# RWKV in two chains with PSUM of their own: inverses of a block and preparation of the next interleaved with the chunks of the preceding one

## The chip, the cores and the metric

The kernel runs on one core of a Trainium2 chip. A core has five engines that run their own instruction streams: TensorE (PE, matrix products, whose results go to PSUM), VectorE (DVE), ScalarE (ACT), GpSimd (POOL) and SyncE (SP), whose queue issues nearly all DMAs here. The metric is the device time of one execution in microseconds (us). Lower is better.

## The reference

One layer of a hybrid trunk, batch 1, 2048 tokens and 16 learned meta tokens ahead of them (2064 in all), width 1024, float32. The normalised input goes through one projection, whose columns feed three head groups:

```python
p = rms_norm(h, norm_mix_pre[l]) @ w_in[l]
pa = p[..., :A_COLS]
pb = p[..., A_COLS:A_COLS + B_COLS]
pc = p[..., A_COLS + B_COLS:]
oa = rg_lru_group(...)               # linear recurrence with gates, 256 columns
ob = forgetting_attention_group(...) # softmax attention with decay, 8 heads of 64
oc, v_own = rwkv7_group(...)         # RWKV-7, 4 heads of 64
mixed = jnp.concatenate([oa, ob, oc], axis=-1) @ w_out[l]
h = h + rms_norm(mixed, norm_mix_post[l])
f = causal_dwconv(rms_norm(h, norm_ffn_pre[l]) @ ffn_up[l], ffn_conv[l])
gate, val = jnp.split(f, 2, axis=-1)
f = (jax.nn.gelu(gate, approximate=True) * val) @ ffn_down[l]
h = h + rms_norm(f, norm_ffn_post[l])
```

The RWKV group is a recurrence over tokens with a 64 x 64 state for each head:

```python
def step(S, inp):
    r_t, w_t, k_t, v_t, kk_t, a_t = inp
    s_kk = jnp.einsum('bhij,bhj->bhi', S, kk_t)
    S = S * w_t[:, :, None, :] - s_kk[..., None] * (kk_t * a_t)[:, :, None, :] + v_t[..., None] * k_t[:, :, None, :]
    return S, jnp.einsum('bhij,bhj->bhi', S, r_t)
```

## The kernel before

The kernel has these stages: the input projection, with gates, RWKV and LRU beside it; the attention, in two halves of its query blocks; the output projection `w_out_tile`, partly beside the second half of the attention; and the two products of the feed-forward block (`ffn_up`, `Down`), which the change doesn't touch.

**Input projection.** The tokens go through in three parts (`w_in_tokens`): two blocks of tokens each, of 400 and 384, 384 and 384, 256 and 256 columns. `w_in_part` (L293) is a generator whose steps are called units here, 25 in a part: first the gates' columns (`w_in_gate`), then 8 units of RWKV's columns ("c"), 4 of the LRU's ("a"), and the keys, values and queries. A unit makes 24 matmuls for each block of tokens into a `psp` tile (five PSUM banks on the left side). The results are stored to DRAM scratch, where the recurrences read them.

**Recurrences beside it.** `Beside` (L1897) holds a generator and a pace: after each unit, `advance` takes PACE steps of it. PACE is 2.0, and the generator of a part, `recurrences` (L1927), is added after READY + 1 = 14 units. What isn't done at a part's end goes on in the next part's units; what is left after the last part is traced by `finish` before the attention. The generator takes the attention's gates (`gate_block`, L377), and then for each of three blocks of 256 tokens (block 8 has 64):

- preparation (`Rwkv.block`, L993): loads of the mixed columns, decay, gates, normalised keys; its results are `rav` (r, -, v), `bk`, `wc`, `bon`, `sg`;
- in `Rwkv.chunks` (L1077) up to `SOLVED`: scores of a chunk's 64 tokens (L1096, masked into `sc` at L1101), their 16 x 16 diagonal blocks through DRAM (`da`, L1114, L1117) into rows on which POOL and DVE solve 15 steps in turn (L1139, L1140), the result back through DRAM (`dx`, L1143), and transposes of `bk` and `rav` (L1125) into `sc` and `w3`;
- then the rest of `chunks` of the *preceding* block, kept as `R.ending`: inverses put together from the 16 x 16 blocks (`small`, L1163), products per chunk (L1203 to L1227), the state from chunk to chunk (L1247), the outputs (L1280, L1284), group norm, and at the end the transposes (L1304), the gate product (L1308) and the store to `scr["mix"]` (L1318);
- the LRU of the block (`lru_block`, L1371), in four steps.

**PSUM of the recurrences.** `ps()` gives tiles of the tag "at" with two buffers (named `rps` in the profile), `pe()` tiles of the tag "ae" with one (named `eps`). Tiles of a tag take its buffers in the order of the program. Preparation, gates and LRU use `pe()`; scores, transposes, chunks and output use `ps()`.

**Order.** A planner with a timeline model sets the order of the instructions on each engine at compile time, from the order of the program as priority and from what is ready by its model. On the chip each engine takes its instructions in that order and waits on semaphores. PSUM and SBUF of the recurrences are on the right side and come free when `rec` closes; weights of W_out take that room in SBUF, and the attention's third bank for maxima (`ps_more`, used from the sixth head of the first half on) that room in PSUM. `meta()` (L579), the attention of the meta tokens, is traced at the half turn of the attention.

## Time and profile before

| what | time |
|---|---|
| runs, median of 3 (lowest to highest) | 3083.14 us (3079.87 to 3085.98) |
| the profiled execution | 3087.03 us |
| its span, from the first to the last instruction | 3085.3 us |
| granted clock of TensorE, mean | 0.964 |

Times on a profile's rows are microseconds from the start of the span unless marked ns. The profile's page has a row for each engine: busy time, share of the span, number of instructions. Below it the span stands in 40 slices of 77.1 us; a digit is the busy share of a slice in tenths, and PEclk the clock that was granted to TensorE, in tenths of full speed. A window's row gives start and end of the stretch, its length, the busy time of each engine (count), then the granted clock, the share of time in which the DMA engines were busy, and what they moved in GB/s. A row of the timeline gives start, length, engine, line, operation, what it writes and reads, and a count of equal ones merged. A row of waits gives who waited for whom: us in total, times, the longest. A fp32 matmul stands as two matmul records. A busy PE is one that has a matmul under way; that doesn't make it PE at its peak.

### The profile page before, as it was taken

The numbers are of one execution on the slowest core, as the hardware profiler recorded it, in microseconds if no ns is written. First come the engines' busy times: TensorE is split into PE (matmuls) and PEld (weight loads), VectorE is DVE, ScalarE is ACT, GpSimd is POOL, SyncE is SP. The second block draws the span as 40 slices with busy tenths as digits, with TensorE's granted clock in tenths as the row PEclk, the third lists the DMA queues.
The fourth block names the chain that finished last, engine by engine and source line by source line (L and its number), as shares of the span: only waits on it lengthen the run. The fifth ranks groups of instructions, "written<-read, shape, count | busy, mean of one in ns | idle before, by whom it ended". The sixth has DMA issues, their size and how long they took to land.

```text
span 3085.3 us, 52708 instructions
## 1 busy us (share of the span) xinstructions
PE 2905.6 (94%) x18470; PEld 2485.8 (81%) x18470; DVE 2127.9 (69%) x4349; ACT 1447.5 (47%) x2783; POOL 1317.4 (43%) x1491
## 2 busy tenths in 40 slices
PE   7999999999989878898989899999999999999998
PEld 6998899888866544565458899999999998787876
DVE  5268544766677867777745788788778776547766
ACT  4245322444335534445534656666566665324333
POOL 1001121122134645546742457445645534556665
PEclk9999999999978979999999999999999999999999
DMA  6776457466653345445235555566777765435444
GB/s 216 244 229 215 148 176 221 153 219 219 192 134 78 91 112 126 109 112 119 61 112 185 166 175 176 178 196 213 216 211 212 217 193 164 167 103 174 145 163 143
DMA packets 463210, 515.78 MB, mean 167 GB/s; under 512 B 84977, under 2 KB 355003, under 8 KB 461393
## 3 DMA queue, kind: packets, MB, share of 16 engines
q1 hardware_dynamic: 462560, 512.03, 55.5%
q8 instruction: 145, 2.38, 0.3%
q14 instruction: 121, 0.98, 0.1%
q0 software_dynamic: 384, 0.39, 0.0%
HBM read 360.73 MB, written 151.56 MB: 166 GB/s over the span
## 4 chain that ended last, share of the span: by engine, by line
PE 39%; DMA 5%; DVE 5%; POOL 3%; issue 2%; ACT 1%; SPq 0%; POOLq 0%; DVEq 0%; ACTq 0%
PE psu L168 9%; PE psu L169 9%; PE psu L170 8%; PE psd L170 2%; PE psd L169 2%; PE psd L168 2%; DMA u<-scr_ff 1%; PE po L696 1%; DMA xt<-scr_h 1%; PE pswo L168 1%; PE pswo L169 1%; PE pswo L170 1%; DVE fo L1571 1%; PE sc L673 1%; DVE uw L1571 1%
## 5 line engine op out<-in xcount | busy, mean ns | idle before, releaser
L168 PE MATMUL psu<-xo,uw 128*128 128x344 f32 x1848 | 591.3, 324 | 16.2 <-ACT xo L1570 6.9
L169 PE MATMUL psu<-xo,uw 128*128 128x344 f32 x1848 | 594.1, 322 | 0.5 <-DVE xo L1571 0.5
L170 PE MATMUL psu<-xo,uw 128*128 128x344 f32 x1848 | 584.3, 320 | 0.0
L170 PE MATMUL psp<-xh,wl 128*128 128x384 f32 (+2 forms) x1152 | 379.1, 330 | 3.8 <-DMA wl<-scr_wk 3.8
L168 PE MATMUL psp<-xh,wh 128*128 128x384 f32 (+2 forms) x1152 | 380.2, 330 | 2.3 <-DMA wh<-scr_wk 2.3
L169 PE MATMUL psp<-xl,wh 128*128 128x384 f32 (+2 forms) x1152 | 377.6, 328 | 0.0
L168 PEld LDWEIGHTS psu<-xo,uw 128*128 128x128 f32 x1848 | 348.1, 189 | 19.5 <-ACT xo L1570 7.1
L1571 DVE TENSOR_TENSOR uw<-uq,uw 128x512 fp32r<-128x512 f32 x341 | 311.1, 918 | 65.3 <-ACT uw L1570 62.4
L169 PEld LDWEIGHTS psu<-xo,uw 128*128 128x128 f32 x1848 | 349.2, 189 | 1.1 <-DVE xo L1571 1.0
L170 PEld LDWEIGHTS psu<-xo,uw 128*128 128x128 f32 x1848 | 347.6, 189 | 0.0
L1570 ACT ACTIVATE uw<-uq 128x512 fp32r<-128x512 f32 x462 | 288.0, 627 | 113.0 <-PE psu L170 53.8
L678 ACT ACTIVATE p<-sc,bias 128x512 f32<-128x512 f32 (+4 forms) x352 | 197.8, 590 | 238.2 <-PE sc L674 181.7
L1701 DVE SCALAR_TENSOR_TENSOR uy<-psu,ffn_cols,uy 128x342 f32<-128x342 f32 (+1 forms) x396 | 223.8, 566 | 67.3 <-ACT uy L1699 65.9
L717 POOL TENSOR_TENSOR acc<-acc,p 128x512 f32<-128x512 f32 (+3 forms) x208 | 223.8, 1082 | 65.2 <-DVE acc L717 40.4
L1707 POOL TENSOR_TENSOR uy<-uy,uy 128x342 f32<-128x342 f32 (+1 forms) x132 | 138.5, 1049 | 256.3 <-DVE uy L1701 72.1
L170 PEld LDWEIGHTS psp<-xh,wl 128*128 128x128 f32 x1152 | 219.5, 191 | 13.3 <-issue 6.3
L1571 POOL TENSOR_TENSOR uw<-uq,uw 128x512 fp32r<-128x512 f32 x121 | 175.6, 1451 | 125.9 <-ACT uw L1570 102.8
L168 PEld LDWEIGHTS psp<-xh,wh 128*128 128x128 f32 x1152 | 219.6, 191 | 8.5 <-issue 3.5
L169 PEld LDWEIGHTS psp<-xl,wh 128*128 128x128 f32 x1152 | 219.3, 190 | 6.8 <-issue 4.8
L548 DVE TENSOR_REDUCE mc<-mx 128x1 f32<-128x400 f32 (+6 forms) x320 | 171.7, 553 | 67.3 <-PE mx L545 62.5
L1571 DVE TENSOR_TENSOR fo<-u,fo 128x896 fp32r<-128x896 f32 x88 | 109.7, 1247 | 122.4 <-ACT fo L1570 122.4
L1570 ACT ACTIVATE fo<-u 128x896 fp32r<-128x896 f32 x88 | 81.1, 922 | 206.2 <-POOL u L1817 111.7
(460 smaller groups left out, 6474.0 us busy)
## 6 DMA issues: line engine op xcount, KB each, us to landing
uq<-scr_us SPq DMA_DIRECT2D x220, 256.0 KB
uq<-in_ffn_up_dram SPq DMA_DIRECT2D x209, 256.0 KB
wl<-scr_wk SPq DMA_DIRECT2D x48, 512.0 KB
wh<-scr_wk SPq DMA_DIRECT2D x48, 512.0 KB
u<-scr_ff SPq DMA_DIRECT2D x88, 256.0 KB
scr_ff<-uy SPq DMA_DIRECT2D x110, 171.0 KB
raw<-in_w_in_dram SPq DMA_DIRECT2D x24, 512.0 KB
scr_wk<-wh SPq DMA_DIRECT2D x24, 512.0 KB
```

Source lines behind the costliest of these rows:

```text
L168: nc.tensor.matmul(out, ah, bh, start=first, stop=False, skip_group_check=more)
L169: nc.tensor.matmul(out, ah, bl, start=False, stop=False, skip_group_check=more)
L170: nc.tensor.matmul(out, al, bh, start=False, stop=last, skip_group_check=more)
L548: self.reduced = nc.vector.tensor_reduce(mc[:rows, i, ci : ci + 1], ps[:rows, :full], axis=AX.X, op=ALU.max)
L673: nc.tensor.matmul(ps[:rows, :w], k1[:, ks : ks + rows], q1[:, c0:n], start=True, stop=False)
L678: last = nc.scalar.activation(p[:rows, :w], ps[:rows, :w], AF.Exp, bias=bias[:rows, j : j + 1])
L696: mm = nc.tensor.matmul(po[at : at + 64, c0:n], v1[:rows, j], p[:rows, : n - c0], start=start and i < 2, stop=end and i + 2 >= len(group), ...
L717: eng.tensor_tensor(a, ps_[0][0][:rows, c0:n] if start and i == 1 else a, p[:rows, : n - c0], op=ALU.add)
L1570: core.nc.scalar.activation(hi, src, AF.Copy)
L1571: (eng or core.nc.vector).tensor_tensor(lo, src, hi, op=ALU.subtract)
L1701: stt(y[:, :n], src[:, i : n + i], cw[:, 44 * i + cc : 44 * i + cc + 1], y[:, :n], op0=ALU.mult, op1=ALU.add)
L1707: core.pooled = nc.gpsimd.tensor_tensor(v[:, :n], g[:, :n], v[:, :n], op=ALU.mult)
```

## The change

- `Rwkv.block` and `chunks` are cut into three generators: `prepare(b)` (2 steps), `inverses(b)` (3 steps) and `chunks(b)` (7 steps), which hand on their tiles in `self.made`.
- Scores, transposes and the output's two products (both in halves of one tile) take `pe()` in place of `ps()`; `ps()` is left to the chunks. The scores are computed for one head group after the other.
- `r` is written into `rav` and multiplied by the decay there, after the bonus has been taken; the tile "r" goes. `sg` has three buffers. The gates' tiles named "r" take the tag "gt".
- `lru_block` has one more yield, and a class `Lru` runs all its blocks as one generator, a block only when its columns are counted in `lru.blocks`.
- `recurrences` prepares the first block of a part and then takes steps by a string, ORDER, for each block: i the inverse of this block, g gates, l LRU, c chunks of the preceding block, a preparation of the next. Six of the seven steps of the part's last chunks follow at its end; the seventh is the next part's.
- READY goes from 13 to 9, PACE from 2.0 to 3.0; GATED = 14 says when the LRU's columns are there.

```diff
@@ Rwkv.prepare (was block) @@
-        sg = self.t([P, nch, CH], "sg", bufs=2)
+        sg = self.t([P, nch, CH], "sg", bufs=3)
...
-        r = self.t([P, m2, CH], "r")
+        rav = self.t([P, m2, 3, CH], "rav", bufs=2)
+        r = rav[:, :, 0]
         self.mixed(0, 0, c0, n, [half(r, 0), half(r, 1)])
-        rav = self.t([P, m2, 3, CH], "rav", bufs=2)
         self.mixed(512, 4, c0, n, [half(rav, p)[:, :, 2] for p in range(2)])
...
-        tt(rav[:, :, 0], r[:], e1, op=ALU.mult)
...
+        tt(r, r, e1, op=ALU.mult)
...
+        self.made[b] = sg, rav, bk, wc, bon
         yield
-        yield from self.chunks(b, nch, sg, rav, bk, wc, bon)
-
-    def chunks(self, b, nch, sg, rav, bk, wc, bon):
+
+    def inverses(self, b):
...
-            pss = [self.ps().rearrange("p (i t) -> p i t", t=P) for _ in range(2)]
-            for i in range(m):
-                for h, ps in enumerate(pss):
-                    hs = slice(64 * h, 64 * h + 64)
+            for h in range(2):
+                hs = slice(64 * h, 64 * h + 64)
+                ps = self.pe().rearrange("p (i t) -> p i t", t=P)
+                for i in range(m):
                     nc.tensor.matmul(
                         ps[:, i], bk[hs, c0 + i].rearrange("p a t -> p (a t)"),
                         rav[hs, c0 + i, 0:2].rearrange("p a t -> p (a t)"), start=True, stop=True,
                     )
-            for h, ps in enumerate(pss):
                 tt(
...
             for src, dst in ((bk, sc), (rav[:, :, 1:3], w3)):
-                ps = self.ps().rearrange("p (c t) -> p c t", t=P)
+                ps = self.pe().rearrange("p (c t) -> p c t", t=P)
...
-        yield self.SOLVED
+        self.made[b] += sc, w3, dx
+        yield
+
+    def chunks(self, b):
...
+        sg, rav, bk, wc, bon, sc, w3, dx = self.made.pop(b)
...
-            ps = self.ps()
+            both = self.pe()
+            ps, pg = both[:, :256], both[:, 256:]
...
-            pg = self.ps()
@@ constants @@
-READY = 13
-PACE = 2.0
+READY = 9
+GATED = 14
+PACE = 3.0
+
+ORDER = "iigglcclicalccclcalll"
@@ recurrences @@
+class Lru:
+    def __init__(self, *args):
+        self.blocks, self.gen = 0, self.steps(*args)
+
+    def steps(self, *args):
+        for b in range(Rwkv.BLOCKS):
+            while b >= self.blocks:
+                yield False
+            for _ in lru_block(*args, b):
+                yield True
+
+    def step(self):
+        return next(self.gen, False)
...
+    todo = ((0, 1, 2), (3, 4, 5), (6, 7, 8))[part]
+    yield from R.prepare(todo[0])
+    gens = {"g": gates(), "c": R.ending}
+    for b in todo:
+        gens["a"] = R.prepare(b + 1) if b < todo[-1] else iter(())
+        gens["i"] = R.inverses(b)
+        for s in ORDER:
+            if lru.step() if s == "l" else next(gens[s], gens[s]) is not gens[s]:
+                yield
+        gens["c"] = R.chunks(b)
+
+    R.ending = gens["c"]
+    for _ in range(6):
+        next(R.ending)
         yield
-    for b in ((0, 1, 2), (3, 4, 5), (6, 7, 8))[part]:
-        gen = R.block(b)
-        while next(gen) != R.SOLVED:
+    if part == 2:
+        yield from R.ending
+        while lru.step():
             yield
-        yield from R.ending
-        R.ending = gen
-        yield from lru_block(core, R, scr, lk, b)
@@ hybrid_block_kernel @@
                 for i, _ in enumerate(units, READY + 1 if part == 0 else 1):
-                    if i == READY + 1:
-                        beside.add(recurrences(core, R, lk, a["fox_f_bias"], scr, blocks, part))
+                    if i == READY + (part == 0):
+                        beside.add(recurrences(core, R, lru, a["fox_f_bias"], scr, blocks, part))
+                    elif i == GATED - 1 + (part == 0):
+                        lru.blocks += 3
                     beside.advance()
...
         beside.finish()
-        for _ in R.ending:
-            pass
         rec.close()
```

More of the change, by code (lines that the diff above doesn't have):

```diff
@@ L389, in gate_block @@
     nc.sync.dma_start(x, scr["f"][:, t0 : t0 + n])
-    a = new("r")
+    a = new("gt")
     nc.scalar.activation(a, x, AF.Abs, bias=core.fb[:])
@@ L405, in gate_block @@
     nc.vector.tensor_copy(core.ctail[:], c[:, n - META :])
-    ch, cl = new("k", F32R), new("r", F32R)
+    ch, cl = new("k", F32R), new("gt", F32R)
     nc.scalar.activation(ch, c, AF.Copy, scale=-1.0)
@@ L953 @@
     BLOCKS = 9
-    SOLVED = "solved"
     @staticmethod
@@ L964, in __init__ @@
         self.nc = core.nc
-        self.ending = ()
+        self.made, self.ending = {}, iter(())
     def t(self, shape, tag, dt=F32, bufs=1):
@@ L991, in mixed, with sizes, prepare @@
             nc.vector.scalar_tensor_tensor(out, v(raw[:, p, :n]), k["mu"][:, cc], out, op0=ALU.mult, op1=ALU.add)
-    def block(self, b):
+    @staticmethod
+    def sizes(b):
         nch = 4 if b < 8 else 1
+        return nch, 2 * nch, 4 * nch
+    def prepare(self, b):
+        nch, m2, _ = self.sizes(b)
         n = CH * nch
-        m2 = 2 * nch
         c0 = PAD + self.start(b)
@@ L1143, in chunks @@
             nc.sync.dma_start(dxv[q], ix[q * nblk : (q + 1) * nblk, : 16 * jw])
-        yield self.SOLVED
+        self.made[b] += sc, w3, dx
+        yield
+    def chunks(self, b):
+        nc, k, core = self.nc, self.k, self.core
+        tt = nc.vector.tensor_tensor
+        nch, m2, ni = self.sizes(b)
+        sg, rav, bk, wc, bon, sc, w3, dx = self.made.pop(b)
         xu = self.t([P, 4, ni, 32], "xu")
@@ L1924, in finish, with recurrences, gates @@
             pass
-def recurrences(core, R, lk, f_bias, scr, blocks, part):
-    for blk in blocks:
-        gate_block(core, R, f_bias, scr, blk[2])
+class Lru:
[9 more added lines that the diff above has]
+        return next(self.gen, False)
+def recurrences(core, R, lru, f_bias, scr, blocks, part):
+    def gates():
+        for blk in blocks:
+            gate_block(core, R, f_bias, scr, blk[2])
+            yield
+    todo = ((0, 1, 2), (3, 4, 5), (6, 7, 8))[part]
[6 more added lines that the diff above has]
+            if lru.step() if s == "l" else next(gens[s], gens[s]) is not gens[s]:
+                yield
+        gens["c"] = R.chunks(b)
+    R.ending = gens["c"]
+    for _ in range(6):
+        next(R.ending)
         yield
-    for b in ((0, 1, 2), (3, 4, 5), (6, 7, 8))[part]:
-        gen = R.block(b)
-        while next(gen) != R.SOLVED:
+    if part == 2:
+        yield from R.ending
+        while lru.step():
             yield
-        yield from R.ending
-        R.ending = gen
-        yield from lru_block(core, R, scr, lk, b)
 _INS = [
```

5 lines of the change are left out of this document (3 added, 2 removed).

## The prediction

> **What bounds the kernel now.** I read the page first, for the engine that is busiest and for where it isn't.
>
> ```profile
> span 3085.3 us, 52708 instructions
> PE 2905.6 (94%) x18470; PEld 2485.8 (81%) x18470; DVE 2127.9 (69%) x4349; ACT 1447.5 (47%) x2783; POOL 1317.4 (43%) x1491
> PE   7999999999989878898989899999999999999998
> PEclk9999999999978979999999999999999999999999
> ```
>
> PE carries the kernel. Its weak stretch is slices 11 to 16 (77 us each), where both busy share and granted clock fall. To name the stages there, three rows: the projections (first and last matmul), the store of the RWKV result, and the batch of meta tokens (`meta()`), which the attention issues at its half turn.
>
> ```profile
> L168 PE MATMUL psp<-xh,wh x1152: 274/337/741, 41.4 to 879.9; 128*128 128x384 f32 x95, 128*128 128x256 f32 x64, 128*128 128x400 f32 x33
> L1318 SPq DMA_DIRECT2D scr_mix<-rwxu x1: 377/377/377, 1139.4 to 1139.4; - x1
> L625 PE MATMUL mx<-p,p x16: 262/263/285, 1141.8 to 1143.4; 16*64 16x16 f32 x16
> ```
>
> So the projections run from 41 to 880, RWKV ends at 1139, and the first half of the attention, from 880 to 1142, shares the core with the last of RWKV. The windows view by these stages (columns: stretch, its length, busy time of PE, weight loads, DVE, ACT, POOL, then the clock):
>
> ```profile
> 41.00:880.00 839.00, 817.06 (x6811) 751.51 (x6811) 473.84 (x1172) 327.65 (x631) 132.35 (x219) 0.98 0.62 198
> 880.00:1142.00 262.00, 218.71 (x1869) 147.86 (x1868) 211.59 (x689) 117.00 (x255) 127.35 (x200) 0.82 0.43 99
> 1400.00:1545.00 145.00, 131.13 (x561) 70.45 (x560) 108.20 (x255) 74.38 (x130) 101.10 (x113) 0.96 0.38 86
> ```
>
> Projections with recurrences beside them: PE busy 97.4% at clock 0.98, a yield of 0.954. Attention with recurrences: 83.5% at 0.82, a yield of 0.685. Attention alone: 90.4% at 0.96, a yield of 0.868. I call busy time times clock the work at full clock: 817.06 x 0.98 + 218.71 x 0.82 = 800.7 + 179.3 = 980.0 us up to the half turn. The change computes the same products, so it can only move this work to a place with a better yield.
>
> How much of RWKV is late? Its PSUM tiles are `rps` (chunks and inverses) and `eps` (preparation, gates, LRU); PE time in the two windows:
>
> ```profile
> 41.00:880.00 839.00, 161.82 (x2904) 0.98 0.62 198
> 880.00:1142.00 262.00, 79.69 (x1258) 0.82 0.43 99
> 41.00:880.00 839.00, 61.06 (x223) 0.98 0.62 198
> 880.00:1142.00 262.00, 9.33 (x40) 0.82 0.43 99
> ```
>
> The first two are `rps`, the others `eps`: 79.69 + 9.33 = 89.0 us are late. Why, the order of time on PE shows (start, length):
>
> ```profile
> 819.91 0.60 PE L1308 MATMUL rps<-rwsg,g_up 128*128 128x256 f32 x2
> 822.33 1.16 PE L1096 MATMUL rps<-rwrav,rwbk 64*128 64x128 f32 x8
> 843.26 1.20 PE L1163 MATMUL rps<-rwxu,rwsc 32*32 32x32 f32 x64
> 920.49 0.59 PE L1308 MATMUL rps<-rwsg,g_up 128*128 128x256 f32 x2
> 921.70 1.16 PE L1096 MATMUL rps<-rwrav,rwbk 64*128 64x128 f32 x8
> 1015.48 0.70 PE L1308 MATMUL rps<-rwsg,g_up 128*128 128x256 f32 x2
> 1016.11 0.71 PE L1096 MATMUL rps<-rwrav,rwbk 64*128 64x128 f32 x4
> 792.74 0.70 DVE L1154 STREAM_TRANSPOSE rwxu<-rwxu 64x512 f32<-64x512 f32 x1 [2.17 <-DMA rwxu<-dx]
> ```
>
> The scores of a block (L1096) start 1 to 2 us after the last gate product (L1308) of the chunks two blocks back: 820 to 822, 921 to 922, 1015 to 1016. And the block whose inverse was transposed at 793 starts its chunks (L1163) only at 843, behind the next block's scores. Two buffers of one PSUM tag serve both, in program order, so scores, inverse and chunks form one chain, with a period of 922 - 822 = 99 and 1016 - 922 = 94 us.
>
> **The change part by part.** *Two chains.* Scores, the two sorts of transposes and the output move to `eps`, one bank; the chunks keep the two `rps` buffers. Chunks alone take 843 to 920, 77 us; the scores and inverses, 822 to 843 and on, lie beside them. The period falls from 94-99 to about 77 us, provided that steps are issued fast enough.
>
> *Issue.* READY 13 to 9 and PACE 2 to 3: in the third part the old schedule has 12 units x 2 = 24 slots after the start for some 47 steps (2 gates and 3 blocks of 4 + 7 + 4); the new one 17 units x 3 = 51 for some 62 (6 preparation, 2 gates, 9 inverses, 1 + 7 + 7 + 7 chunks, some 23 LRU). Left behind the projections: about 30 steps before (47 - 24 and the last block's 7), 11 after. Constants and gates come earlier; the cover is an idle DVE (57% busy above).
>
> *What is still late.* In the third part, 17 of 25 units last 17/25 x 240 us (the part's stretch 640 to 880) = 163, with the moved work some 210. RWKV there needs preparation and first inverse, about 70 us (estimate from 822 to 843 doubled, with the preparation before it), two periods of 77 and a quarter block at about 45: 270. So 60 us run beside the attention instead of 259 (1139 - 880), and 89.0 x 60/259 = 21; I take 25 us. Moved: (89.0 - 25) x 0.82 = 52.5 us at full clock. Each moved block also brings some 23 DMA issues (0.4 us each by the store above) into SP's queue, past the weight loads: 3 blocks, 28 us of a queue that runs through 839; PE waits there for `wh` and `wl` only this much now:
>
> ```profile
> PE psp L170 <- DMA wl<-scr_wk: 3.8, 4, 1.4
> PE psp L168 <- DMA wh<-scr_wk: 2.3, 3, 1.0
> ```
>
> *Going to and fro on PE.* Small matmuls use part of the array. Around one excursion from the projections:
>
> ```profile
> 863.17 0.28 PE L170 MATMUL psp<-xh,wl 128*128 128x256 f32 x1
> 863.29 0.28 PE L168 MATMUL psp<-xh,wh 128*128 128x256 f32 x1
> 863.50 1.13 PE L1021 MATMUL eps<-rwwa,wa_up 64*128 64x256 f32 x4
> 866.75 0.39 PE L169 MATMUL psp<-xl,wh 128*128 128x256 f32 x1
> 866.97 0.28 PE L170 MATMUL psp<-xh,wl 128*128 128x256 f32 x1
> 867.09 0.28 PE L168 MATMUL psp<-xh,wh 128*128 128x256 f32 x1
> ```
>
> Projection matmuls follow each other at 0.12 us; into the excursion it takes 0.21, and the first one back takes 0.22: 0.2 us an excursion. The code has some 34 PSUM tiles in a block, 280 in all; three streams in place of two cut finer. Bounds: nothing (the groups stay together), or 280 x 0.2 = 56 us (each alone, none before). Whole runs of small matmuls still stand together in these rows (L1021, and x64 of L1163), so I take 50 more excursions, 10 us. The Trainium skill, TensorEngine Tiling (Array Packing), section Tiling Modes, says that a change of the tiling mode, not of the tile, drains the array; the rows above agree. The same section of the Trainium skill says that tiles work independently of each other; that speaks against the new order of the scores.
>
> That order takes one head group after the other, where the old one alternates them:
>
> ```profile
> 525.04 1.16 PE L1096 MATMUL rps<-rwrav,rwbk 64*128 64x128 f32 x16
> 530.19 1.17 PE L1096 MATMUL rps<-rwrav,rwbk 64*128 64x128 f32 x16
> 729.30 1.16 PE L1096 MATMUL rps<-rwrav,rwbk 64*128 64x128 f32 x8
> ```
>
> Alternated, 16 take 1.16 us; in the later block (and at 822 and 921) the schedule has already put 8 by 8, in the same 1.16. So 2.3 us a block are lost in at most five blocks: 0 to 12 us, I take 5.
>
> *Small ones.* `r` in place of its own tile, `gt` for the gates, a third `sg`, one more yield in the LRU: no instruction more; they order writes behind the chunks' last reads, on DVE and ACT, which have room until 880. Bounds 0 and 2 us a block on the preparation, off PE; I take 0. One output bank for two products makes ACT wait for the second (0.6 us by L1308), behind nothing on PE.
>
> **The sum.** Projections: 800.7 + 52.5 + 15 = 868.2 at 0.954 give 910 us, an end at 951 (now 880). To the half turn remain 980.0 - 853.2 = 126.8: 60 us with RWKV at 0.685 do 41, the other 86 at 0.868 take 99. The half turn comes at 951 + 159 = 1110, not 1142: **32 us less**. After it nothing changes. On the profiled execution (3087.0 us with what lies around its span) that is 3055; that execution is 3.9 us over the median of the runs, so I give **3051 us**.
>
> Ends: no extra cost and all of the rest at 0.868: 853.2/0.954 = 894, 126.8/0.868 = 146, half turn at 1081, 61 less: 3022. All of the rest at 0.685: 910 + 185, half turn at 1136, 6 less: 3077. Full price of excursions and pairs: 921/0.954 = 965, + 159, half turn at 1165, 23 more: 3106.
>
> **Rivals.** *A finer cut, or waits that move into the projections (slower).* The place is PE's queue between 41 and 951: a static order there puts an unready small matmul ahead of the projections. It costs 0.2 us an excursion, or the wait itself. It decides from 32 x 0.954/0.2 = about 150 more excursions, or when PE's idle share in the stage passes 6% (now 2.6%; 3.4% of 910 is 31 us). Against it: the longest wait of PE now is 4.7 us (second row below). For it: beside the attention the same steps do stall PE. At the full price 3106.
>
> ```profile
> PE mx L563 <- DVE rwgsm L76: 4.9, 1, 4.9
> PE rps L1125 <- DVE rwbk L1119: 5.2, 2, 4.7
> ```
>
> *Attention without its filler yields no more than now (same).* If its own chain from maximum to score limits it, 0.685 stays: 3077. For it: its first half has the shorter rows of keys. Against it: 0.868 at 1400 to 1545, and DVE at 211.59 of 262, part of which is RWKV's.
>
> *The two chains are none (same).* If one `eps` bank becomes the ring, the period stays near 95 us and RWKV stays as late: 3083. Against it: all of `eps` holds PE for 70 us in 9 blocks, 8 us a block; with scores, transposes and evictions I reckon a third of the period.
>
> *More comes back (faster).* If excursions stay few and the clock rises as soon as RWKV is out, 3022; the loads of W_out, which take RWKV's room in SBUF, then also come before the half turn.
>
> **How the numbers follow.** Forecast 0.45, its own range 3030 to 3072; more 0.17; attention no better or one chain, together 0.14; slower 0.24. A measurement of this kernel tells about 0.2% (6 us) from no change: faster 0.62, same 0.14, slower 0.24. The range takes in 3022 with some ten us for the W_out loads, and most of the way to 3106: 3012 to 3098.
>
> **What would show it.** Right: last projection matmul near 951, the RWKV store near 1010, the row of L625 near 1110, under 30 us of `rps` after the projections, clock over 0.9 between. Scores no longer start behind L1308. Wrong: PE's idle share before the last projection over 6%, scores still 94 us apart, or the half turn's row not earlier though RWKV's store is.

## The result, and the profile after

The changed kernel takes **3133.7 us** (median of 4 runs, 3125.3 to 3140.5) against 3084.6 us (4 runs, 3079.9 to 3089.5) for the kernel before on the same chip: a ratio of **1.0158**, with a 95% interval of 1.0126 to 1.0190. It is slower by 1.6%; the forecast was 3051 us, and the range ended at 3098.

The page of the changed kernel, the same lines as of before: span, busy time of the first engines, and PE's busy share and clock in 40 slices (now of 78.4 us).

```profile
span 3135.9 us, 52724 instructions
PE 2940.1 (94%) x18470; PEld 2510.1 (80%) x18470; DVE 2131.4 (68%) x4349; ACT 1452.5 (46%) x2783; POOL 1305.4 (42%) x1491
PE   7999999999997787999889899999999999999998
PEclk9999899999996888999999999999999999999999
```

The weak stretch is shorter, four slices in place of six, but it begins later and its first slice has a clock of 0.6. The number of matmuls is the same; PE's busy time grew by 34.5 us. Last projection matmul, RWKV's store and the half turn of the attention, from the view of single lines:

```profile
L168 PE MATMUL psp<-xh,wh x1152: 274/337/747, 42.2 to 934.7; 128*128 128x384 f32 x95, 128*128 128x256 f32 x64, 128*128 128x400 f32 x33
L1329 SPq DMA_DIRECT2D scr_mix<-rwxu x1: 390/390/390, 1069.5 to 1069.5; - x1
L625 PE MATMUL mx<-p,p x16: 262/263/281, 1192.7 to 1194.3; 16*64 16x16 f32 x16
```

The projections end 54.8 us later (879.9 to 934.7). RWKV ends 70 us *earlier* (1139.4 to 1069.5), as the change wants. And the half turn comes 50.9 us later all the same (1141.8 to 1192.7). From the half turn to the end nothing changed: 3135.9 - 1192.7 = 1943.2 us, before 3085.3 - 1141.8 = 1943.5. So the loss lies ahead of the half turn, and all of it is there when the projections end: from there to the half turn it took 262 us before and takes 258 now.

The windows view by these two stages, first all engines, then `rps` and `eps` alone (columns as in the prediction):

```profile
42.00:935.00 893.00, 874.75 (x7482) 798.59 (x7480) 503.91 (x1272) 339.39 (x655) 135.77 (x239) 0.97 0.58 187
935.00:1193.00 258.00, 194.55 (x1198) 124.42 (x1197) 190.44 (x597) 118.60 (x239) 121.02 (x179) 0.77 0.48 120
...
42.00:935.00 893.00, 144.83 (x3136) 124.65 (x3136) 65.39 (x147) 22.60 (x49) 0.97 0.58 187
935.00:1193.00 258.00, 42.11 (x560) 35.13 (x560) 12.92 (x34) 4.15 (x10) 0.77 0.48 120
...
42.00:935.00 893.00, 134.99 (x661) 88.50 (x661) 51.26 (x103) 52.12 (x104) 0.97 0.58 187
935.00:1193.00 258.00, 17.79 (x68) 11.69 (x68) 6.93 (x16) 7.90 (x20) 0.77 0.48 120
```

Read the first pair by busy time times clock, as in the prediction. The projections do 874.75 x 0.97 = 848.5 us of work with a yield of 0.95, as before. The stage from their end to the half turn does 194.55 x 0.77 = 149.8 us, 29.5 less than the 179.3 of before, and takes the same time: its yield fell from 0.685 to 0.58. RWKV's PE time beside the projections grew from 161.82 + 61.06 = 222.9 to 144.83 + 134.99 = 279.8 us, by 56.9, and their end moved by 54.8: one for one. Only 29.1 us of the 56.9 left the later stage (89.0 before, 42.11 + 17.79 = 59.9 now). The other 27.8 are new: RWKV's PE time in both stages rose from 311.9 to 339.7 us for the same matmuls.

Two more changes show in the order of time. The first ending of the attention (L743, the sum of a query block's weights), before:

```profile
936.50 0.48 PE L743 MATMUL mx<-oh,ones_col 128*1 128x512 f32 x1
```

and after:

```profile
1028.77 0.40 PE L743 MATMUL mx<-oh,ones_col 128*1 128x512 f32 x1
...
699.19 1.16 PE L1100 MATMUL eps<-rwrav,rwbk 64*128 64x128 f32 x8
793.87 1.16 PE L1100 MATMUL eps<-rwrav,rwbk 64*128 64x128 f32 x8
896.28 1.16 PE L1100 MATMUL eps<-rwrav,rwbk 64*128 64x128 f32 x8
```

The lead-in of the attention, from the last projection matmul to that ending, grew from 57 to 94 us. And the scores of the blocks are still 95 and 102 us apart.

RWKV's last product into PSUM is done before 1070. What is left up to the half turn is the first half of the attention with no matmul of RWKV beside it (same columns as above):

```profile
1070.00:1193.00 123.00, 88.31 (x384) 49.26 (x383) 84.00 (x242) 56.51 (x107) 72.47 (x105) 0.84 0.56 142
```

Its yield is 88.31 x 0.84 / 123 = 0.60, where the prediction took 0.868 for the attention alone.

### The profile page after: what moved, and what is told of

It is laid out like the page before. It is cut to its first block, busy times and chain, and to the rows that moved or that the text cites. A ratio compares the mean times of both kernels' runs of the same rounds, so it can differ in the third digit from the quotient of the medians.

```text
span 3135.9 us, 52724 instructions
## 1 busy us (share of the span) xinstructions
PE 2940.1 (94%) x18470; PEld 2510.1 (80%) x18470; DVE 2131.4 (68%) x4349; ACT 1452.5 (46%) x2783; POOL 1305.4 (42%) x1491
## 5 line engine op out<-in xcount | busy, mean ns | idle before, releaser
L548 DVE TENSOR_REDUCE mc<-mx 128x1 f32<-128x400 f32 (+5 forms) x320 | 171.9, 553 | 84.8 <-PE mx L545 83.0
```

Of the source, the lines that this page charges most:

```text
L548: self.reduced = nc.vector.tensor_reduce(mc[:rows, i, ci : ci + 1], ps[:rows, :full], axis=AX.X, op=ALU.max)
```

## The experiments

Each ratio is against runs of the kernel before on the same chip, whose medians were 3085 to 3088 us. "Stage" is the stretch from the last projection matmul to the half turn. Times and ratios are from the runs, the other columns from the profiled ones; work is busy PE time times clock in the stage, yield is work by length. A profiled execution can lie up to 9 us off the median of the runs (held16: 3073.3 against 3081.9), so the columns of one row needn't add up to its time.

| kernel | time, us (runs) | ratio, 95% interval | last projection | stage | work in it, yield | half turn | half turn to end |
|---|---|---|---|---|---|---|---|
| before | 3087 | 1 | 880 | 262 | 179, 0.69 | 1141.8 | 1943.5 |
| after | 3133.7 (4) | 1.0158 (1.0126-1.0190) | 935 | 258 | 150, 0.58 | 1192.7 | 1943.2 |
| fast_one_chain | 3086.9 (10) | 1.0007 (0.9990-1.0024) | 901 | 246 | 169, 0.69 | 1147.2 | 1933.5 |
| old_pace | 3162.6 (4) | 1.026 (1.0239-1.0281) | 886 | 326 | 182, 0.56 | 1211.9 | 1948.4 |
| psum_only | 3186.9 (4) | 1.034 (1.0318-1.0362) | 881 | 364 | 190, 0.52 | 1244.7 | 1941.1 |
| order_only | 3128.2 (4) | 1.0111 (1.0081-1.0142) | 914 | 272 | 167, 0.61 | 1186.0 | 1943.0 |
| no_tail | 3107.0 (1) | - | 934 | 228 | 123, 0.54 | 1162.0 | 1943.3 |
| psum_wide | 3136.6 (1) | - | 874 | 300 | 186, 0.62 | 1174.5 | 1959.8 |
| spread | 3136.6 (4) | 1.0146 (1.0116-1.0176) | 935 | 259 | 149, 0.58 | 1193.7 | 1938.4 |
| held20 | 3130.6 (4) | 1.0134 (1.0101-1.0168) | 930 | 255 | 149, 0.58 | 1185.4 | 1942.6 |
| after_wide | 3132.3 (4) | 1.0132 (1.0103-1.0161) | 932 | 269 | 150, 0.56 | 1200.8 | 1923.5 |
| before_wide | 3070.3 (6) | 0.9939 (0.9913-0.9964) | 881 | 262 | 183, 0.70 | 1143.6 | 1924.9 |
| later | 3095.1 (10) | 1.0016 (1.0002-1.0030) | 849 | 310 | 202, 0.65 | 1159.1 | 1926.8 |
| later_held | 3089.5 (10) | 1.0010 (0.9996-1.0025) | 849 | 303 | 194, 0.64 | 1152.2 | 1935.4 |
| held16 | 3081.9 (10) | 0.9982 (0.9964-1.0000) | 912 | 241 | 172, 0.71 | 1153.1 | 1918.5 |
| held16_five | 3128.7 (1) | - | 906 | 269 | 166, 0.62 | 1175.4 | 1951.5 |
| held16_old_banks | 3113.6 (7) | 1.0089 (1.0063-1.0115) | 908 | 275 | 173, 0.63 | 1183.1 | 1928.1 |
| held14 | 3098.4 (6) | 1.0035 (1.0016-1.0055) | 901 | 271 | 179, 0.66 | 1172.6 | 1926.4 |

### Order, pace and banks apart

*old_pace*: the changed kernel at the old start and pace.

```diff
-READY = 9
-GATED = 14
-PACE = 3.0
+READY = 13
+GATED = 15
+PACE = 2.0
```

> The changed kernel with its two chains, but at the old pace (READY 13, PACE 2, GATED 15). Theory P (place: PE is full beside the projections, so RWKV moved there costs its PE time, and the attention's first half does not give it back): RWKV is late again, last projection at 880 to 905, time 3070 to 3095. Theory C (the new chains themselves cost: one bank, the scores' order, the finer cut): last projection still past 920 or the half turn past 1175, time over 3115.

*fast_one_chain*: the kernel before with `PACE = 3.0`.

> The kernel before with PACE 3 in place of 2 and nothing else. Theory P: more RWKV lies beside the projections, last projection at 900 to 930, time 3095 to 3130. Theory C: the single chain limits RWKV whatever the pace, last projection within 15 of 880, time 3075 to 3095.

*psum_only*: the kernel before with scores, transposes and output on `pe()`.

```diff
-            pss = [self.ps().rearrange("p (i t) -> p i t", t=P) for _ in range(2)]
-            for i in range(m):
-                for h, ps in enumerate(pss):
-                    hs = slice(64 * h, 64 * h + 64)
+            for h in range(2):
+                hs = slice(64 * h, 64 * h + 64)
+                ps = self.pe().rearrange("p (i t) -> p i t", t=P)
+                for i in range(m):
...
-            ps = self.ps()
+            both = self.pe()
+            ps, pg = both[:, :256], both[:, 256:]
```

> The kernel before with only the PSUM of the scores, transposes and output moved to the one-buffer tag, at the old order and pace. Theory P: little changes, time 3070 to 3095, as the pace keeps RWKV late. Theory C: 3100 or more. If the shared buffers were what tied the chain, the scores of a block no longer start within 3 us behind the gate product of two blocks before.

*order_only*: the reverse, the changed kernel with these three back on `ps()`, the scores alternated as before.

> The new order, pace and start (READY 9, PACE 3, three generators), with scores, transposes and output back on the two rps buffers and the scores alternated as before. Theory, the moved work costs its own PE time: the order decides, whatever the banks; the last projection matmul is at 925-940, the lead-in of the attention 80-95 us, the half turn at 1180-1200, the time 3120-3140 us (3133.7 with the banks of the change). Rival, the banks cost it: with two alternating buffers the result is that of the old order at the new pace, 3080-3095 us. Either way the period from scores to scores shows what the bank of its own gave: 94-102 us says nothing, 110 or more that the two chains were worth something.

A faster pace alone moves the projections' end 20 us back (theory P) and shortens the stage by 15, and its time is the same as before within 0.2% (theory C). The new order and pace alone (order_only) cost 1.1%, against 1.6% for the whole change (the intervals overlap): most of the loss comes without the new banks. It comes in another way, though: in order_only the projections end at 914, 34 us later, and not at the 925 to 940 that I gave. RWKV's PE time beside them grew by only 13.8 us (to 236.7), PE's idle time there by 12.7, from 21.9 of 839 in before to 34.6 here:

```profile
41.00:914.00 873.00, 838.39 (x7030) 765.76 (x7029) 486.62 (x1205) 329.11 (x634) 131.59 (x222) 0.97 0.61 191
```

The changed kernel has less idle time (18.3) and more PE time. The distances of the scores, 146, 67 and 89 us, say nothing clear on the banks by the sign that I had set. In psum_only the scores no longer start behind the output of two blocks back, but they lie 119 to 130 us apart: untied from that output, the chain did not get shorter.

The banks without the new pace cost more than the change itself (2.6 and 3.4%), and in another place: in old_pace the endings of the attention stand still from 1057.2 to 1139.5, in psum_only from 1057.0 to 1175.2. PE at the end of that stillness, in psum_only:

```profile
1169.36 0.69 PE L1307 MATMUL eps<-rwsg,g_up 128*128 128x64 f32 x2
1171.80 0.56 PE L545 MATMUL mx<-k,q 128*128 128x272 f32 x1 [1.75 <-DVE rwxu L1315]
```

The first row is the last product of RWKV into `eps`; the second is a maximum of the attention, and what released it is DVE's reading of that product. old_pace has the same two rows (its first maximum after the gap starts at 1136.14, released by DVE's L1327). The attention's third bank for maxima, used from the sixth head on, is the room that `eps` leaves. Before, the last user of `eps` was an LRU block near 1040; with the output on `eps` it is the very last step of RWKV. The next two kernels test it.

### The inherited bank

`WIDE` names the half and the head, counted from 0, from which the third bank is used. *psum_wide*: psum_only with the third bank from the second half of the attention on. *held16_five*: the kernel held16 (below, whose RWKV ends late) with the third bank back at the sixth head; all that is left of RWKV is then traced ahead of that head too, and its store comes at 1098.6 in place of 1145.6.

```diff
-WIDE = (0, 5)
+WIDE = (1, 0)
```

> The PSUM part alone (scores, transposes and output on eps, order and pace of before), and the attention's third bank for maxima used from the second half on instead of from the sixth head. Theory, third bank: that bank is the one that eps leaves, and with the output on eps its last user is RWKV's last product, so in the run of the PSUM part alone the maxima of the sixth head waited until 1171.7 and the endings stood still from 1057.0 to 1175.2. Without the third bank in the first half no two endings are over 40 us apart there, the half turn falls from 1244.7 to 1140-1170 and the time from 3186.9 to 3085-3115 us. Rival, starved chain: the endings stood still because the chunks of RWKV, slowed by scores of 13-18 us a block on one bank, held PE and DVE; then the gap stays over 80 us and the time at 3170-3190.

> held16 with the third bank from the sixth head on, as in the kernels before and after. Theory, inherited bank: its RWKV ends near 1145, eps is its last user, so the sixth head's maxima wait for it: a gap of 60-90 us between two endings ahead of the half turn, the half turn at 1190-1225, the time at 3115-3150 us against 3081.9. Rival: the chip doesn't wait there (RWKV's output is long done when the sixth head's maxima come), no gap over 55 us, 3075-3095 us.

In psum_wide the longest time between two endings ahead of the half turn is 38 us, the half turn comes 70 us earlier (1174.5, where I gave 1140 to 1170), and 50 us of the 100 lost are back. The time stays above what I gave (3085 to 3115): RWKV's store comes only at 1214.8, behind the half turn, and there the wait comes back. No ending lies between 1155.0 and 1235.5, and this maximum of the second half starts 1.2 us after RWKV's last product into `eps` (1213.01, 0.69 us long):

```profile
1214.91 0.77 PE L545 MATMUL mx<-k,q 128*128 128x512 f32 x1 [1.22 <-DVE rwxu L1315]
```

In held16_five the stillness returns, from 1042.7 to 1102.1, and ends the same way (the half turn, 1175.4, comes earlier than the 1190 to 1225 that I gave; the time is in the range):

```profile
1096.81 0.69 PE L1323 MATMUL eps<-rwsg,g_up 128*128 128x64 f32 x2
1098.72 0.56 PE L545 MATMUL mx<-k,q 128*128 128x272 f32 x1 [1.22 <-DVE rwxu L1331]
```

That the third bank waits for RWKV's last step is shown by these rows and by the stillness going and coming with it. In the changed kernel RWKV ends early enough (1069.5), and no such gap stands there: it explains the two kernels, and why the new pace is needed with the new banks, but not the loss of the change.

### The attention without RWKV

*no_tail*: the changed kernel without the chunks and the output of blocks 7 and 8; `bon` is stored in place of the output. What it leaves out is most of what RWKV does beside the attention.

```diff
+        if b >= 7:
+            n = CH * nch
+            t0 = self.start(b)
+            for _ in range(6):
+                yield
+            nc.sync.dma_start(
+                self.scr["mix"][768:1024, t0 : t0 + n].rearrange("(p r) t -> r p t", r=P),
+                bon[:].rearrange("p (a c) t -> p a (c t)", a=2),
+            )
+            yield
+            return
```

> The changed kernel without the chunks and output of RWKV's blocks 7 and 8, which it leaves out (their place in the mixed tensor gets the bonus alone). One look at the attention with almost no RWKV beside it. Theory P (the first half of the attention is bound by itself): from the last projection to the half turn still 230 us or more (258 in the changed kernel). Theory S (the start: RWKV's rest at half clock holds the attention up): 205 us or less, and no stretch of half clock over 20 us after the projections.

The window of the stage, and who waited for whom in its main part, 991 to 1162 (us in total, times, longest):

```profile
934.00:1162.00 228.00, 155.56 (x614) 88.02 (x612) 168.48 (x508) 107.08 (x213) 117.14 (x174) 0.79 0.54 133
...
POOL p L680 <- ACT p L678: 32.6, 25, 3.8
ACT p L678 <- PE sc L674: 25.3, 16, 5.5
...
PEld sc L673 <- ACT p L678: 19.9, 29, 2.0
...
DVE mc L548 <- PE mx L545: 13.9, 12, 4.5
```

This is the run that decides, one execution, 2 us under the 230 us of theory P and far from the 205 of theory S. With almost no RWKV beside it, the first half of the attention takes 228 us for 155.56 x 0.79 = 122.9 us of work: a yield of 0.54, not 0.87; the changed kernel's own stretch without RWKV, 1070 to 1193, agrees (0.60). So the forecast's 159 us could not be had by moving RWKV away, since 228 remain without nearly all of it. No engine is full (PE 155.56 of 228, DVE 168.48); scores (`sc`), exponentials (`p`) and maxima (`mx`, `mc`) wait for each other in turn. How much of the low yield is waiting and how much the granted clock (0.79) wasn't taken apart.

Before, 89.0 us of RWKV's PE time lay in this stage; in no_tail 12.9 are left, and it is 262 - 228 = 34 us shorter: 34/76 = 0.45 for each us of RWKV, where it cost 1 beside the projections. This price isn't fixed. Against no_tail's own kernel, the changed one, it is 30/47 = 0.64 (258 us with 59.9 of RWKV); fast_one_chain pays 18/63 = 0.29 (246 us with 75.7), and held16, below, 13/55 = 0.23 (241 us with 68.3).

### Does the long lead-in cost?

*spread*: the remaining recurrences traced two steps behind each of the attention's pieces in place of ahead of it.

> The changed kernel with what is left of the recurrences after the last part not traced ahead of the attention but two steps behind each of its first ten pieces (8 heads of 2 query blocks), the rest ahead of the sixth head. Theory, PE's queue: in the lead-in (934.7 to 1028.8, 94 us) the first maxima (957.7, 962, 967.5, 973, 979) each stood behind RWKV's chunk products, which the order had put first; with the attention first the lead-in falls to 55-70 us, the half turn from 1192.7 to 1155-1170, the time to 3095-3110 us. Rival, clock or loads: the lead-in is long because PE runs at half clock and the loads of keys and queries come late whatever the order; then it stays at 85-95 us and the time at 3125-3140. Second rival, RWKV becomes the end: spread out it ends later, and the sixth head's third bank, which eps leaves, waits for it: a gap of over 40 us between endings and 3125 or more.

PE's order came out as in the changed kernel, record for record, so this says nothing of the order. It shows that the lead-in is no accident of one execution (93.4 us, half turn 1193.7). *held20* takes the steps away from the end of the projections and ties them to the attention's endings (what is left at the sixth head is traced ahead of it):

```diff
-                    beside.advance()
+                    if part < 2 or i < 20:
+                        beside.advance()
...
+                    if len(self.steps) >= 1:
+                        with self.core.tc.issue_after(self.steps[-1].ins):
+                            for _ in range(steps):
+                                beside.step()
```

> The changed kernel; in the third part no step of the recurrences is taken after the 19th unit, and the rest is issued behind the attention's first ending, three steps behind each further piece. RWKV's matmuls behind the projections are as many as in the changed kernel, but 17 instead of 251 of them stand on PE ahead of the attention's 31st. (The run before with two steps behind each piece had the changed kernel's order on PE, all 18470 records, so it said nothing of this order.) Theory, backlog: the lead-in takes 56-62 us with 11-22 us of RWKV's PE time in it and 82-94 us with 42-48, some 1.3 us for each us above 20; with 17 matmuls ahead it falls from 93.6 to 58-66 us, RWKV costs about 0.4 of its PE time later (16 us), and the half turn comes at 1170-1182 instead of 1192.7, the time at 3108-3124 us. Rival, the stage has one length: whatever lies first, attention and RWKV share an engine; lead-in shorter, half turn within 5 us of 1192, 3128-3138 us. Second rival, RWKV becomes the end: the sixth head's third bank waits for it, a gap of over 40 us between endings, 3140 or more.

First ending and stage of held20, by timeline and windows:

```profile
994.56 0.40 PE L743 MATMUL mx<-oh,ones_col 128*1 128x512 f32 x1
...
930.00:1185.00 255.00, 193.02 (x1198) 117.67 (x1197) 190.99 (x597) 118.52 (x239) 120.10 (x177) 0.77 0.50 122
```

The lead-in fell to 64 us, as given. The half turn came only 7 us earlier, 5 of them by the projections' earlier end, and the stage stayed at 255 us: near to the rival (half turn within 5 us, 3128 to 3138). The lead-in is where RWKV's rest showed, not what it cost.

### RWKV later

*later*: the kernel before, the third part's recurrences five units later, WIDE = (1, 0). *later_held*: the same, held as in held20 from unit 22 on.

```diff
-                    if i == READY + 1:
+                    if i == (READY + 1 if part < 2 else 19):
```

> The kernel before with the opposite of the change in one place: the third part's recurrences start five units later (after 19 units instead of 14), so that more of RWKV lies beside the attention; and the third bank for maxima from the second half on, since eps comes free later. Theory, RWKV costs its own PE time beside the projections and about 0.4 of it beside the attention (262 us with 89 us of RWKV's PE time before, 228 us with almost none): some 25 us of PE time move, the last projection matmul comes at 850-858, the half turn at 1120-1135, the time at 3065-3080 us against 3084 before. Rival, chain: RWKV's period of 94-99 us a block makes it end last, its store at 1165 or later, and the half turn or W_out waits for it: 3085-3110. Second rival, the third bank is worth something itself in the first half: the endings of the last three heads stand further apart than before and the time is 3084-3095.

> The kernel before with the third part's recurrences five units later (848.9, 91 us of lead-in, half turn 1159.1, 3095.1 us), and now no step of them after the 21st unit, the rest behind the attention's first ending, three steps behind each further piece: 16 RWKV matmuls instead of 250 ahead of the attention's 31st. Theory, backlog: lead-in 58-66 us instead of 91, the half turn at 1125-1145, the time at 3065-3082 us, the first below the kernel before. Rival, RWKV is the end: it ends after 1190, the half turn to the end takes longer than 1945 us, and the time is 3090 or more.

*held16* and *held14*: the changed kernel, held from unit 16 or 14 on, three and four steps behind each piece, WIDE = (1, 0).

> As the kernel held from the 20th unit on, but from the 16th on, so that about half as much again of RWKV is late (483 matmuls in place of 321), and with the third bank for maxima from the second half on. Theory, RWKV costs its own PE time beside the projections and about 0.4 of it beside the attention once the lead-in is free: some 25 us of PE time move, the last projection matmul comes 20-28 us before the 934.9 of the changed kernel, the half turn at 1150-1168, the time at 3090-3108 us. Rival, chain: RWKV ends after 1180 and holds the W_out stage, half turn to end longer than 1950 us, time 3115-3140.

> held16 with no step of the third part's recurrences after the 13th unit in place of the 15th, and four steps behind each of the attention's pieces: 579 RWKV matmuls late in place of 483, none ahead of the attention's 31st. Theory, the stage has room: from the last projection matmul to the half turn it took 258 us in the changed kernel and 241 in held16 although PE's work in it (busy time by clock) went from 150 to 172 us; 10-15 us more leave the projections (an end at 895-903 in place of 912.1), the stage takes 240-255, the half turn comes at 1138-1153, the time at 3062-3080 us. Rival, chain: RWKV's last blocks end after 1165 and hold the W_out stage, as where the recurrences of the kernel before start five units later (309 us in the stage); half turn after 1155, 3085 or more.

The controls: *after_wide* and *before_wide* differ from the two kernels by WIDE alone, *held16_old_banks* from held16 as order_only does from the changed kernel.

> The changed kernel with the attention's third bank for maxima from the second half on, nothing else: the control for held16, which was 52 us below the changed kernel with its last projection matmul 23 us earlier, the half turn 40 us earlier (1153.1) and the rest after the half turn 25 us shorter (1918 against 1943 us). Theory, place of RWKV: what held16 gained up to the half turn is its later RWKV, and the third bank only shifts work of the last three heads across the half turn; then the half turn is at 1180-1200, the last projection matmul at 930-938, the time at 3120-3137. Rival, the bank: the third bank in the first half is itself worth a loss of 20-30 us, and after_wide is at 3100-3115 us, most of held16's gain.

> The kernel before with the third bank for maxima from the second half on: the control for the two kernels with recurrences five units later (3095.1 and 3089.5 us). Theory, place of RWKV: the bank moves the time by under 6 us, 3080-3092 us, and the later start of RWKV, which brought the last projection matmul 30 us forward, was paid back beside the attention (309 and 303 us from there to the half turn against 262). Rival, the bank: 3060-3075 us, the bank alone is a gain and the later start a loss of 20 us or more; or 3095 and above, the bank a loss that hid what the later start gained.

> held16 with scores, transposes and output back on the two rps buffers, the scores alternated as before: what the banks of the change are worth once RWKV is late again. Theory, the banks give nothing: some 555 matmuls late in place of 483, half turn within 10 us of held16's 1153, the time at 3072-3092 us. Rival, two chains: without them RWKV ends 20 us or more after held16's 1145.6 and holds W_out, 3095 us or more. Second rival, one bank is too few: alternating buffers are faster, 3060-3070 us.

held16, the projections and the stage by windows:

```profile
41.00:912.00 871.00, 849.00 (x7180) 776.14 (x7179) 487.90 (x1215) 329.39 (x635) 131.77 (x223) 0.98 0.60 192
912.00:1153.00 241.00, 197.57 (x1509) 124.79 (x1507) 204.34 (x651) 118.27 (x250) 123.95 (x194) 0.87 0.46 111
```

the stage of after_wide:

```profile
932.00:1201.00 269.00, 204.81 (x1204) 128.03 (x1202) 194.24 (x602) 119.48 (x239) 118.72 (x179) 0.73 0.46 116
```

and the stage of later:

```profile
849.00:1159.00 310.00, 256.00 (x2209) 173.72 (x2208) 245.02 (x772) 140.49 (x298) 132.17 (x214) 0.79 0.37 88
```

With the third bank in the same place, held16 is 50 us below after_wide (3081.9 against 3132.3): the projections end 20 us earlier, and the stage, with 22 us *more* of work in it, is 28 us shorter. So RWKV's place (how much of it stands where, and behind which piece of the attention) accounts for 50 of the 62 us between before_wide and after_wide. The clock granted in the stage was 0.87 in held16 and 0.73 in after_wide; which of the two, the fuller PE or the higher clock, brought the other isn't shown. The other controls correct my other readings:

- before_wide is 0.6% faster than the kernel before, half turn unmoved, the rest 19 us shorter; I had expected no change. So later and later_held, which looked like the kernel before, are losses of 25 and 19 us against their control: 32 us fewer beside the projections, 41 to 48 more in the stage (in later_held RWKV's store comes only at 1220.1, behind the half turn). The price of 0.45 doesn't hold on: in these two, whose control has 183 us of work in the stage, what was moved into it cost 1.3 to 1.5 times what it saved.
- held16_old_banks is 32 us above held16, its RWKV store at 1179 in place of 1146. Once RWKV is late, the two chains are worth something; in the changed kernel, where it is early, they bring RWKV's store forward (1126.0 in order_only, 1069.5 with them) but not the time.
- held14, with a little more of RWKV late and four steps behind each piece, lost 16 us on held16. I had expected a gain; the half turn behind RWKV's store at 1162.6 speaks for the rival that RWKV's chain sets the end, but no run tests that by itself.

The best of all is before_wide, the kernel before with one constant changed: 3070.3 us. What the third bank costs after the half turn wasn't taken further; on the changed kernel the same constant shortened the rest by 20 us too, but put the half turn 8 us later, and the median fell by only 1.4 (the profiled execution is 6 us under it).

## Why the prediction was wrong

**The step that failed** is the last one of the sum: "the other 86 at 0.868 take 99". It took the yield of the attention alone at 1400 to 1545, in its second half, for the first half. There the attention with almost no RWKV yields 0.54 (no_tail; 0.60 behind RWKV's end in the changed kernel itself), and the 0.685 of before needed RWKV, which filled part of its waits. The work was forecast well in sum: 868.2 + 126.8 = 995 us to the half turn, measured 848.5 + 149.8 = 998. The 159 us for what remained behind the projections were 258. Of the 99 us between, the 23 us of work that stayed behind beyond the forecast explain about a third (an estimate: 23 at a yield of 0.685 are 34 us); the rest is the yield. Taking 29.5 us of work out of a stage that waits for itself gave back 4 us, and what was put beside the full projections cost all of itself.

Point by point:

- *Projections, 910 us, an end at 951.* Mechanism right, size 16 us too large: 893 us, an end at 935, at a yield of 0.95 against 0.954. That it came so near is in part luck, as two terms missed in opposite ways: 29.1 us of RWKV's PE time were moved in place of 89.0 - 25 = 64, and 27.8 us were new in place of 15. Not all of the 27.8 is the change's order: held20, with the same number of RWKV's matmuls in both stages, has 322.6 us of RWKV's PE time in place of 339.7. Beyond the scores (next point) it wasn't taken apart.
- *Excursions 10, lost pairs 5.* The scores' matmuls, from 41 to 1230, PE's busy time in before:

```profile
41.00:1230.00 1189.00, 31.05 (x264) 25.89 (x264) 0.94 0.57 172
```

  in the changed kernel:

```profile
41.00:1230.00 1189.00, 40.32 (x264) 33.50 (x264) 0.92 0.55 169
```

  and in order_only, where the pairs are back:

```profile
41.00:1230.00 1189.00, 27.82 (x264) 23.23 (x264) 0.92 0.56 169
```

  So the lost pairs cost 9.3 us against before and 12.5 against order_only, at the upper end of 0 to 12 and about twice what I took. The 0.2 us for each excursion wasn't measured by itself.
- *Rival "a finer cut, or waits that move into the projections".* The sign was right, the mechanism not: PE is idle 18.3 us of 893 there (2.0%), less than the 2.6% of before. The projections grew by work, not by waits; in order_only, with the old banks, waits did move in (34.6 us of 873, 4.0%). The Trainium skill, Perfetto Trace Analysis, section Optimization Strategies, gives the highest possible utilization of the matmul engine as the general goal; here PE's busy share beside the projections rose from 97.4 to 98.0% and the kernel became slower, so the measurement decides against reading that share by itself.
- *Rival "attention without its filler yields no more than now".* This was the right one, at 0.14 with another. Its price was still too kind: it kept 0.685 for the rest, and the yield fell to 0.58.
- *Period 94-99 to 77 us.* It stayed at 95 and 102. The scores no longer stand behind the output two blocks back, but with the scores of a block spread over 12 to 24 us on one bank (6 to 10 before, from the first to the last matmul's start), the rival "the two chains are none" had some truth. held16 against held16_old_banks shows that the banks aren't worthless.
- *RWKV's store near 1010, 25 us of its PE time late.* It came at 1069.5, with 42.11 + 17.79 = 59.9 us late.
- *After the half turn nothing changes.* Right, 1943.2 against 1943.5 us.
- *The lead-in* had no step in my sum, and held20 shows that it needn't have one: with 64 us in place of 94 the stage is as long.

What stays open: why the first half of the attention yields so little by itself was narrowed to waits between its own engines at a lower clock, not taken apart; why held16 does more work in a shorter stage than the changed kernel; and why the third bank in the first half makes the stages behind it longer.

## What to carry to other kernels

Ask of each stage what a us of moved work costs *there*: measure the stage without its filler (leave the work out in one run) before taking work away from it, and don't lend it the yield of a stage that looks alike. Here the stage at 97% busy took the added PE time one for one, and the one that waits for itself gave back 4 us for 29.5 us of work less; the price there ran from 0.23 to about 1.5 us for each us, by how RWKV lay in it, so one price doesn't serve for the next step. And when a tile moves to another buffer, look who inherits that buffer: its last user sets when the next stage may begin.

## What the runs showed of the hardware

PE can be busy and stay at half clock. Behind the projections of the changed kernel the windows of 10 us read (busy PE, loads, DVE, ACT, POOL, clock):

```profile
955.00:965.00 10.00, 10.00 (x122) 7.95 (x117) 9.49 (x31) 1.16 (x2) 0.00 (x0) 0.50 0.75 198
965.00:975.00 10.00, 10.00 (x54) 7.92 (x55) 4.24 (x16) 4.43 (x10) 0.00 (x0) 0.50 1.04 217
975.00:985.00 10.00, 10.00 (x47) 8.00 (x47) 6.76 (x21) 6.06 (x11) 1.66 (x4) 0.50 0.38 70
```

and three rows of the timeline there show RWKV's small matmuls, and a wait of PE for which the profile has no releaser:

```profile
939.81 1.09 PE L1174 MATMUL rps<-rwxu,rwsc 32*32 32x32 f32 x32
952.57 3.06 PE L1174 MATMUL rps<-rwxu 32*32 32x32 f32 x76 [7.61 <-issue]
959.21 1.91 PE L1174 MATMUL rps<-rwxu,rwsc 32*32 32x32 f32 x32
```

Beside the projections of before, 64 of them took 1.20 us (843.26 in the prediction, where the stage's clock is 0.98); here 32 take 1.09 and 1.91. PE's records fill 955 to 985 without a gap, mostly RWKV's matmuls (26.0 of the 30 us write `rps` or `eps`), many on part of the array, and the clock stays at 0.50. The Trainium skill, TensorE: Matmul & The Clock Gate, Part 1, says that the clock returns to full after a busy window of about 3.4 us; 30 us of records without a gap didn't bring it back, so the measurement differs from the page if busy means the profile's busy time. What the gate counts, and the cause of the 7.61 us, weren't tried by themselves.
